# First weights between the quarters of the input, gate products behind the first pair: a start-up order of a DeltaNet and attention trunk on one core

## Chip, core and metric

The kernel runs on one core of a Trainium2 chip. The metric is the device time of one execution in microseconds; three runs of the kernel before gave a median of 649.35 us (648.83 to 649.79).

## What is computed

Two decoder layers over 256 tokens of width 1024, all in float32. Layer 0 mixes tokens with a gated DeltaNet, layer 1 with attention; each is followed by a squared-ReLU MLP. The change lies in the first sub-layer, whose beginning is:

```
def gated_deltanet(hn, w_in, conv_w, a_log, dt_bias, out_norm_g, w_out):   # hn = rmsnorm(x, g)
    proj = hn @ w_in                                                       # 1024 -> 4*1024 + 16
    qkv = silu(causal_depthwise_conv(proj[..., :3 * 1024], conv_w))
    z = proj[..., 3 * 1024:4 * 1024]
    b_raw, a_raw = proj[..., 4096:4104], proj[..., 4104:]                  # 8 heads each: the gates
    q, k = l2norm(heads of qkv) ...
    beta = sigmoid(b_raw); g = -exp(a_log) * softplus(a_raw + dt_bias)
    o = chunk_gated_delta_rule(q, k, v, g, beta)                           # decay = exp of differences of cumsum(g)
    o = rmsnorm(o, out_norm_g) * silu(z)
    return o @ w_out
```

## The kernel before

**Weights.** All large matrices lie in HBM as one stream of 200 units of 128x1024 floats (512 KB), in the order in which they are used. `prep(u)` (L105) loads a unit into one of three buffers `wf` from SyncE's queue, then ScalarE rounds it to `wh` (L115, "cast") and VectorE forms the rest `wl = wf - wh` (L116, "split"). The first eight units are loaded, cast and split in halves. `wh` and `wl` have five buffers each. A buffer `wf` is loaded again once its split is done, so unit u+3 is issued behind the split of unit u; a buffer `wh` is cast again once TensorE has used it, so the cast of unit u+5 waits for the products of unit u.

**Products.** `mm3` (L128) makes each float32 product of three TensorE products: wh*xh, wh*xl, wl*xh. The input is h0 (x transposed: 8 blocks of 128 features by 256 tokens, loaded in four quarters of two blocks). `Norm.feed` (L166) makes of one quarter, with the norm's weight, `n_h` (ScalarE, L169) and `n_l` (VectorE, L170), squares it (ScalarE, L174 or L177) and adds the square to `n_acc` (VectorE, L178). `Norm.finish` (L180) sums `n_acc` on TensorE (`n_ps`), takes the inverse root in small VectorE steps down to `n_col` (L189), and spreads it over the partitions by TensorE (`n_pb`) and ScalarE (`n_bc`). The norm's factor is applied behind the projections, so the products needn't wait for it.

**A pair.** `pair` (L196) projects 256 output columns, one head's k and q, from two units: 48 products into one PSUM bank. Pairs share the three "acc" banks. What follows for head n (`do_kq`, L499) is the convolution: VectorE multiplies the bank by `n_bc` into `cin` (L478, which frees the bank), ScalarE makes the first tap (L482), VectorE the other three for two blocks (six operations at L484); then a tanh or SiLU, four transposes on TensorE (`kqt`, L517) and squares on ScalarE (L519). `project_gates` (L387) makes the 16 gate columns of plain float32 products of h0 (`ba_ps`, L395), and `make_gates` (L400) the decays of them, by some 25 small VectorE operations. `head_decay` (L453) makes a head's decay matrix: two VectorE operations `ms` (L463), three TensorE transposes `row`, three exponentials.

**Order.** Two strings set the order of the program. `START` (L44) is the order of the first loads, preps and feeds: a token of two signs is a load and its queue (p = `par`, the small parameters; b = `wba`, the gate weights; c = the first constants, with the identity; 0 to 3 = quarters of x; s = SyncE's queue, a = ScalarE's), w is `prep` of the next unit, f is `feed` of the next quarter. `ORDER` (L47) is the order of the mixer's steps: G gates' products, N norm, M gates, L and C two later loads of constants (`sel` and the rest of `con`), kn a pair's products, Kn its convolution, Dn a decay, then v, z, u, i, r, o. The pair k5 comes second and its convolution K5 far behind, so that its bank is held and the others go round in two. From this program a scheduler sets the order of each engine's instructions; every engine then works in its order, and waits in place.

Of the kernel before, what the change touches and what calls it, by code (L numbers as in the profile page):

```python
# [40 lines left out]
}  # L41


START = "pa 0s 1s 2s 3s ba f f w w f f ca"  # L44


ORDER = (  # L47
    "G L k0 N k5 M K0 k3 D0 k2 K2 k1 D6 D2 K3 k4 D1 K1 s0 u2 u0 D3 k6 C K4 D4 D7 u3 u1 K6 i0 k7 K5 K7 v1 "
    "s1 u4 u6 D5 u5 u7 z0 i1 v0 r0 v3 o0 v2 r1 z1 o1"
)  # L50

# [24 lines left out]
def trunk_kernel(ctx: ExitStack, tc: tile.TileContext, xT, wst, wba, par, con, selc, gfin, out):  # L76
# [293 lines left out]
    nprep = nfeed = 0  # L370
    for st in START.split():
        if st == "w":
# [595 lines left out]
```

## Time and profile before

| | |
|---|---|
| median of three runs | 649.35 us |
| the profiled execution | 651.13 us, of which 649.3 us span |
| TensorE busy | 634.4 us, 98% of the span, granted clock 0.996 |
| VectorE busy | 453.7 us, 70%; 8 tenths or more in every slice from 16 to 146 us |
| ScalarE busy | 345.1 us, 53% |
| chain that ended last | TensorE 85%, VectorE 5%, ScalarE 5%, DMA 4%, issue 1% |
| HBM read | 107.51 MB, 167 GB/s over the span |

Busy shares are over the whole span; the change lies in its first tenth. A TensorE row can be "busy" while it waits inside a pipelined stretch, so in that tenth the reader should go by start times and by what ended each idle time. In timelines the bracket behind a row gives the engine's idle time before it, and what released it.

### The profile page before, as it was taken

How to read it: one execution, taken by the hardware profiler on the slowest of the kernel's cores; microseconds unless marked ns; L12 is line 12 of the kernel's file. 1: busy time of each engine (PE TensorE's matmuls, PEld its weight loads, DVE VectorE, ACT ScalarE, POOL GpSimd, SP SyncE). 2: the span in 40 equal slices, each digit the busy share in tenths (PEclk: the TensorE clock that was granted, in tenths of full speed). 3: DMA queues.
4: the chain of work that ended last, by engine and by line, in shares of the span. 5: the costliest groups of instructions: out<-in, count | busy, mean ns of one | idle time of the engine just before them, and what ended most of it. 6: DMA issues, size and time to landing. Idle time of an engine off the chain costs nothing.

```text
span 649.3 us, 13944 instructions
## 1 busy us (share of the span) xinstructions
PE 634.4 (98%) x5754; PEld 608.5 (94%) x5754; DVE 453.7 (70%) x841; ACT 345.1 (53%) x570; POOL 4.0 (1%) x10
## 2 busy tenths in 40 slices
PE   8999999999999999999999999999999999999995
PEld 6988887978999999999999999889999999999995
DVE  5999998997797666645554757775877776545443
ACT  6679873463566666634443444552656555434331
POOL 1000000000000000000000000000000000000000
PEclk9999999999999999999999999999999999999998
DMA  7754253252456565666565655555556666556641
GB/s 259 238 187 130 66 163 100 68 163 66 152 160 185 195 194 195 193 196 194 195 195 195 190 166 163 162 163 162 157 160 204 196 196 195 163 195 195 195 132 65
DMA packets 32031, 109.46 MB, mean 169 GB/s; under 512 B 3552, under 2 KB 3936, under 8 KB 31968
## 3 DMA queue, kind: packets, MB, share of 16 engines
q1 hardware_dynamic: 31248, 107.71, 52.5%
q8 instruction: 45, 0.74, 0.5%
q10 hardware_dynamic: 720, 0.86, 0.4%
q14 instruction: 18, 0.15, 0.1%
HBM read 107.51 MB, written 1.05 MB: 167 GB/s over the span
## 4 chain that ended last, share of the span: by engine, by line
PE 85%; DVE 5%; ACT 5%; DMA 4%; issue 1%; ACTq 0%; DVEq 0%
PE ps_last L136 12%; PE ps_up_m L132 8%; PE ps_up_m L133 8%; PE ps_up_m L130 8%; PE ps_dn_m L133 4%; PE ps_dn_m L132 4%; PE ps_dn_m L130 4%; PE ps_vn L136 3%; DMA wf<-in_w 3%; PE ps_z L136 3%; DVE wl L116 2%; PE ps_qk L132 2%; PE ps_qk L133 2%; PE ps_qk L130 2%; ACT wh L115 2%; PE kk L136 2%
## 5 line engine op out<-in xcount | busy, mean ns | idle before, releaser
L116 DVE TENSOR_TENSOR wl<-wf,wh 128x1024 fp32r<-128x1024 f32 (+1 forms) x208 | 244.3, 1182 | 141.0 <-ACT wh L115 140.4
L115 ACT CAST wh<-wf 128x1024 fp32r<-128x1024 f32 (+1 forms) x208 | 209.7, 1017 | 235.8 <-PE ps_up_m L132 63.7
L130 PE MATMUL ps_up_m<-n_h,wh 128*128 128x256 f32 x512 | 141.6, 277 | 0.5 <-ACT n_h L169 0.5
L132 PE MATMUL ps_up_m<-n_l,wh 128*128 128x256 f32 (+1 forms) x516 | 141.9, 276 | 0.0
L133 PE MATMUL ps_up_m<-n_h,wl 128*128 128x256 f32 x512 | 141.8, 277 | 0.0
L130 PEld LDWEIGHTS ps_up_m<-n_h,wh 128*128 128x128 f32 x512 | 96.1, 188 | 0.7 <-ACT n_h L169 0.7
L132 PEld LDWEIGHTS ps_up_m<-n_l,wh 128*128 128x128 f32 x516 | 96.6, 188 | 0.0
L133 PEld LDWEIGHTS ps_up_m<-n_h,wl 128*128 128x128 f32 x512 | 96.1, 188 | 0.0
L130 PE MATMUL ps_dn_m<-hh_m,wh 128*128 128x256 f32 x256 | 70.7, 276 | 0.0
L132 PE MATMUL ps_dn_m<-hl_m,wh 128*128 128x256 f32 x256 | 70.7, 276 | 0.0
L133 PE MATMUL ps_dn_m<-hh_m,wl 128*128 128x256 f32 x256 | 70.7, 276 | 0.0
L136 PE MATMUL ps_last<-wl,hh_m 128*128 128x256 f32 x226 | 61.9, 276 | 0.0
L136 PE MATMUL ps_last<-wh,hl_m 128*128 128x256 f32 x224 | 61.9, 276 | 0.0
L136 PE MATMUL ps_last<-wh,hh_m 128*128 128x256 f32 x224 | 61.8, 276 | 0.0
L130 PEld LDWEIGHTS ps_dn_m<-hh_m,wh 128*128 128x128 f32 x256 | 48.0, 188 | 0.0
L132 PEld LDWEIGHTS ps_dn_m<-hl_m,wh 128*128 128x128 f32 x256 | 48.0, 188 | 0.0
L133 PEld LDWEIGHTS ps_dn_m<-hh_m,wl 128*128 128x128 f32 x256 | 48.0, 188 | 0.0
L136 PEld LDWEIGHTS ps_last<-wl,hh_m 128*128 128x128 f32 x226 | 42.3, 188 | 0.0
L136 PEld LDWEIGHTS ps_last<-wh,hh_m 128*128 128x128 f32 x224 | 42.1, 188 | 0.0
L136 PEld LDWEIGHTS ps_last<-wh,hl_m 128*128 128x128 f32 x224 | 42.0, 188 | 0.0
L130 PE MATMUL ps_kq<-n_h,wh 128*128 128x256 f32 x128 | 36.6, 286 | 0.0
L130 PE MATMUL ps_qk<-n_h,wh 128*128 128x256 f32 x128 | 36.3, 284 | 0.0
(278 smaller groups left out, 1292.1 us busy)
## 6 DMA issues: line engine op xcount, KB each, us to landing
wf<-in_w SPq DMA_DIRECT2D x192, 512.0 KB, 3.5
wf<-in_w SPq DMA_DIRECT2D x16, 256.0 KB, 4.2
h<-in_x SPq DMA_DIRECT2D x4, 256.0 KB, 6.5
gf<-in_g SPq DMA_DIRECT2D x1, 512.0 KB, 4.0
out<-hg SPq DMA_DIRECT2D x2, 256.0 KB, 2.1
out<-hg ACTq DMA_DIRECT2D x2, 256.0 KB, 2.5
sel<-in_sel SPq DMA_DIRECT2D x1, 448.0 KB, 4.9
cn<-in_con SPq DMA_DIRECT2D x1, 276.0 KB, 4.9
```

What stands on the lines that cost most here:

```text
L115: nc.scalar.copy(wh[:, s], wf[:, s])
L116: nc.vector.tensor_sub(wl[:, s], wf[:, s], wh[:, s].bitcast(F32))
L130: nc.tensor.matmul(o, wh, xh, start=start, stop=False, skip_group_check=True)
L132: nc.tensor.matmul(o[:, s], wh, xl[:, s], start=False, stop=False, skip_group_check=True)
L133: nc.tensor.matmul(o, wl, xh, start=False, stop=stop, skip_group_check=True)
L136: nc.tensor.matmul(o, l, r, start=start, stop=stop, skip_group_check=True)
```

## The change

The first two units are prepared between the quarters of x: load quarter 0, unit 0, quarter 1, feed both, unit 1, then quarters 2 and 3. The first constants move from ScalarE's queue to SyncE's, behind x. In `ORDER` the pair k0 comes before the gates' products G, the norm N follows G, and the load L of `sel` stands behind k5.

```
-START = "pa 0s 1s 2s 3s ba f f w w f f ca"
+START = "pa ba 0s w 1s f f w 2s 3s f f cs"
 ORDER = (
-    "G L k0 N k5 M K0 k3 D0 k2 K2 k1 D6 D2 K3 k4 D1 K1 s0 u2 u0 D3 k6 C K4 D4 D7 u3 u1 K6 i0 k7 K5 K7 v1 "
+    "k0 G N k5 L M K0 k3 D0 k2 K2 k1 D6 D2 K3 k4 D1 K1 s0 u2 u0 D3 k6 C K4 D4 D7 u3 u1 K6 i0 k7 K5 K7 v1 "
     "s1 u4 u6 D5 u5 u7 z0 i1 v0 r0 v3 o0 v2 r1 z1 o1"
 )
```

The scheduler moves more than the strings show. On SyncE's queue, from its first load (wf_111 and wf_96 are unit 0 before and now, h_72 is x), before:

```order
L114 DMA wf_111<-in_w 128x512
L379 DMA h_72<-in_x 128x512 x4
L114 DMA wf_111<-in_w 128x512
L114 DMA wf_120<-in_w 128x512 x2
L742 DMA sel<-in_sel 128x896
L114 DMA wf_165<-in_w 128x512 x2
```

and now:

```order
L114 DMA wf_96<-in_w 128x512
L379 DMA h_72<-in_x 128x512
L114 DMA wf_96<-in_w 128x512
L379 DMA h_72<-in_x 128x512
L114 DMA wf_118<-in_w 128x512 x2
L379 DMA h_72<-in_x 128x512 x2
L379 DMA cn<-in_con 128x384
L114 DMA wf_152<-in_w 128x512 x2
```

The last quarter of x was the fifth load of this queue and is now the eighth; the first constants follow it, and unit 2 (wf_165 before, wf_152 now) follows them without `sel` ahead.

On VectorE, from the split of unit 10 (wl_486) to the multiplications that free the banks of k3 (ps_kq_411) and k2 (ps_kq_483), before:

```order
L116 TENSOR_TENSOR wl_486<-wf_484,wh_485 128x1024
L431 SCALAR_TENSOR_TENSOR gt_p<-gt_p,gt_z 128x16
L478 TENSOR_TENSOR cin_147<-ps_kq_411,n_bc 128x2x256
L433 SCALAR_TENSOR_TENSOR gt_u<-gt_p,gt_u 128x16
L437 SCALAR_TENSOR_TENSOR gt_g<-gt_u,ea 128x16
L116 TENSOR_TENSOR wl_516<-wf_514,wh_515 128x1024
L442 COPY gt_gc<-gc_ps 128x16
L478 TENSOR_TENSOR cin_148<-ps_kq_483,n_bc 128x2x256
```

and now, from the same split on (wl_516, wl_570 and wl_600 are units 11 to 13, L510 with th_554 is head 2's):

```order
L116 TENSOR_TENSOR wl_486<-wf_484,wh_485 128x1024
L116 TENSOR_TENSOR wl_516<-wf_514,wh_515 128x1024
L478 TENSOR_TENSOR cin_148<-ps_kq_483,n_bc 128x2x256
L463 TENSOR_SCALAR ms_629<-cn,gt_gc 128x128
L116 TENSOR_TENSOR wl_570<-wf_568,wh_569 128x1024
L484 SCALAR_TENSOR_TENSOR y_kq_545<-cin_148,pm,y_kq_545 128x256 x6
L463 TENSOR_SCALAR ms_629<-cn,gt_gc 128x128
L463 TENSOR_SCALAR ms_639<-cn,gt_gc 128x128
L116 TENSOR_TENSOR wl_600<-wf_598,wh_599 128x1024
L510 SCALAR_TENSOR_TENSOR kq_386<-th_554,y_kq_545 128x2x128 x2
L463 TENSOR_SCALAR ms_639<-cn,gt_gc 128x128
L478 TENSOR_TENSOR cin_147<-ps_kq_411,n_bc 128x2x256
```

Before, k3's bank was freed first, one small step behind the split of unit 10; now k2's is, right behind the split of unit 11, and k3's comes behind head 2's convolution. The rest of the gates' chain (L431 to L442) and the decay of head 0 now stand ahead of this piece. On TensorE the pair k1 (ps_kq_567), which follows k2's, took k3's bank before and takes k2's now.

On TensorE the end of k2's pair now reads:

```order
L136 MATMUL gc_ps<-gt_g,cn 128x16
L132 MATMUL ps_kq_483<-n_l,wh_309 128x256
L133 MATMUL ps_kq_483<-n_h,wl_310 128x256
L130 MATMUL ps_kq_483<-n_h,wh_309 128x256
L517 MATMUL kqt_402<-cn,kq_386 128x128
L136 MATMUL gl_ps<-gt_gc,cn 128x8
L132 MATMUL ps_kq_483<-n_l,wh_309 128x256
L133 MATMUL ps_kq_483<-n_h,wl_310 128x256
L130 MATMUL ps_kq_483<-n_h,wh_309 128x256
L517 MATMUL kqt_402<-cn,kq_386 128x128 x3
L464 MATMUL row_474<-cn,ms_473 128x128 x2
L465 MATMUL row_474<-cn,gt_gc 128x128
```

Eleven products of k2 and then those of k1 follow. Before, kqt_402 stood some 16 products earlier than gc_ps, and gl_ps and row_474 stood within k1.

## Rows read from the trace of the kernel before

**Rows 1.** Busy time in stretches of 8 us: PE, PEld, DVE, ACT, POOL, clock, DMA, GB/s.
```profile
0.00:8.00 8.00, 5.70 (x18) 3.95 (x20) 2.16 (x7) 3.69 (x7) 3.00 (x8) 1.00 0.68 210
8.00:16.00 8.00, 7.40 (x60) 6.03 (x58) 6.98 (x14) 7.33 (x17) 0.00 (x0) 1.00 0.88 306
```

**Rows 2.** What TensorE waited for in 0 to 200 us: us, times, longest.
```profile
PE kqt L517 <- DVE kq L510: 1.6, 2, 0.8
...
PE ps_z L136 <- DVE cin L478: 0.3, 1, 0.3
```

**Rows 3.** Timeline of TensorE, start: start, length, operation, [idle before <- releaser].
```profile
1.25 4.94 PE L136 MATMUL warm<-wu 128*128 128x256 f32 x12 [1.25 <-DVE wu L358]
9.71 0.63 PE L136 MATMUL ba_ps<-h,sz 128*32 128x256 f32 x4
10.27 0.39 PE L130 MATMUL ps_kq<-n_h,wh 128*128 128x256 f32 x1
16.03 0.95 PE L136 MATMUL n_ps<-ones,n_acc 128*128 128x1 f32 x8
```

**Rows 4.** Timeline of ScalarE, start.
```profile
3.83 0.62 ACT L115 CAST wh<-wf 128x512 fp32r<-128x512 f32 x1 [1.14 <-DMA wf<-in_w]
5.38 0.91 ACT L169 ACTIVATE n_h<-h,pm 128x256 fp32r<-128x256 f32 x2 [0.93 <-DMA h<-in_x]
7.84 0.91 ACT L169 ACTIVATE n_h<-h,pm 128x256 fp32r<-128x256 f32 x2 [1.04 <-DMA h<-in_x]
10.34 0.62 ACT L115 CAST wh<-wf 128x512 fp32r<-128x512 f32 x1 [0.67 <-DMA wf<-in_w]
```

**Rows 5.** DMA issues of 0 to 30 us: KB each, median us from issue to landing.
```profile
wf<-in_w SPq DMA_DIRECT2D x3, 512.0 KB, 4.4
...
cn<-in_con ACTq DMA_DIRECT2D x1, 192.0 KB, 7.2
```

**Rows 6.** Timeline of VectorE, 8 to 22 us.
```profile
8.39 0.88 DVE L170 SCALAR_TENSOR_TENSOR n_l<-h,pm,n_h 128x256 fp32r<-128x256 f32 x2 [1.38 <-ACT n_h L169]
14.59 0.69 DVE L178 TENSOR_TENSOR n_acc<-n_acc,n_sq 128x512 f32<-128x512 f32 x1
15.20 2.49 DVE L116 TENSOR_TENSOR wl<-wf,wh 128x512 fp32r<-128x512 f32 x4
21.68 0.16 DVE L189 TENSOR_SCALAR n_col<-n_y 128x2 f32<-128x2 f32 x1
```

**Rows 7.** Timeline of VectorE, 29 to 45 us.
```profile
29.35 1.21 DVE L116 TENSOR_TENSOR wl<-wf,wh 128x1024 fp32r<-128x1024 f32 x1
36.88 0.68 DVE L478 TENSOR_TENSOR cin<-ps_kq,n_bc 128x512 f32<-128x512 f32 x1
37.63 0.47 DVE L463 TENSOR_SCALAR ms<-cn,gt_gc 128x128 f32<-128x128 f32 x2
39.26 1.22 DVE L116 TENSOR_TENSOR wl<-wf,wh 128x1024 fp32r<-128x1024 f32 x1 [1.16 <-ACT wh L115]
40.41 2.46 DVE L484 SCALAR_TENSOR_TENSOR y_kq<-cin,pm,y_kq 128x256 f32<-128x256 f32 x6
43.92 0.75 DVE L510 SCALAR_TENSOR_TENSOR kq<-th,y_kq 128x256 f32<-128x256 f32 x2
```

**Rows 8.** Timelines of SyncE's queue and of ScalarE: unit 12's issue and cast.
```profile
32.28 0.33 SPq L114 DMA_DIRECT2D wf<-in_w  x1
...
38.18 1.05 ACT L115 CAST wh<-wf 128x1024 fp32r<-128x1024 f32 x1 [1.87 <-DMA wf<-in_w]
```

**Rows 9.** Timeline of TensorE: first of k1, first kqt of head 2, kqt of head 3.
```profile
36.10 0.28 PE L130 MATMUL ps_kq<-n_h,wh 128*128 128x256 f32 x1
44.39 0.33 PE L517 MATMUL kqt<-cn,kq 128*128 128x128 f32 x1 [0.80 <-DVE kq L510]
50.26 0.66 PE L517 MATMUL kqt<-cn,kq 128*128 128x128 f32 x4 [0.16 <-ACT kq L513]
```

**Rows 10.** Busy time and clock just behind TensorE's last product (columns as in Rows 1).
```profile
642.00:644.00 2.00, 0.00 (x0) 0.00 (x0) 1.93 (x12) 1.12 (x3) 0.00 (x0) 0.95 0.00 0
```

## Prediction

> **What bounds the kernel now.** I read the busy times by stretch first, then TensorE's waits, then the timelines of the first 52 us. After the start TensorE is never short of work for long: already in 8 to 16 us 7.40 of 8 us are busy [rows 1], and the largest named wait, for head results of VectorE, is two times 0.8 us [rows 2]. Its clock is at the upper of its two levels (1.00, 2.4 GHz) from the start. So the span is TensorE's work plus what it waits, and only two things can move it here: when it begins to work on weights, and new or vanished waits while VectorE and the transfers set the pace (up to about 50 us).
>
> The start [rows 3]: twelve warm-up rows until 6.19, gates' products whenever a quarter of x lands, and the first weight product at 10.27. From there 48 products take 5.76 us (0.12 each) and `n_ps` starts at 16.03. The early time is spent waiting for transfers: ScalarE waits 0.93, 1.04 and 0.67 us for x and for the second half of unit 0 [rows 4], VectorE 1.38 us behind it [rows 6].
>
> **Landing times.** Before, loads of 256 KB on SyncE's queue land in this order: unit 0's half by 3.83, quarters 0 and 1 by 5.38 and 7.84 [rows 4], quarter 3 by 9.71 [rows 3], unit 0's other half by 10.34 [rows 4]. That is 0.63 us a load at the end of the list, and more before it. The first constants, 192 KB on ScalarE's queue, were under way for 7.2 us of that time [rows 5]; at the 306 GB/s of 8 to 16 us [rows 1], taking them away gives about 0.6 us. By place in the queue, less that 0.6: now quarter 0 lands at 5.3, unit 0's second half at 7.2, quarter 1 at 8.5, unit 1 at 9.1 and 9.7, quarters 2 and 3 at 10.4 and 11.0. So the last quarter comes 1.3 us later than before. Bounds: 11.6 if the constants cost nothing, about 9.7 (as before) if bandwidth is spare.
>
> [...]
>
> **The head.** From quarter 1 on VectorE is dense. It starts on it when `n_h` is there, 0.55 after 8.5. Then, in the new order: three pairs of `n_l` (0.88 a pair, [rows 6]), three additions (0.61, start to start in [rows 6]), unit 1's two splits and unit 2's two (2.49 for four): 2.64 + 1.83 + 2.49 = 6.96, so unit 2 is split at 16.0. Before it was at 15.20 + 1.25 = 16.45. TensorE does the first 12 products from 6.2 and has 36 left from 9.1: 4.3 us, plus eight gate products. Those go at 0.24 to 0.31 each (two in 0.63, [rows 3]), 2.1 us, and before they were hidden in the waits for x. That makes 15.5 against 16.03. Both leads agree: **0.5 us**, with bounds of 0 (quarter 3 at 11.6) and 1.3 (at 9.7). The load of unit 5 waits for unit 2's split and `n_col` for unit 5's: 21.68 [rows 6] becomes 21.2. The moved `sel` and second constants leave the queue ahead of unit 2 and unit 4 and land long before use; I cost them at nothing, and should they delay unit 5 by their 448 KB, the 0.5 is gone.
>
> **The middle.** k1's pair began at 36.10 [rows 9], on k3's bank, free for some time. Now it needs k2's bank, which VectorE frees behind the split of unit 11. That multiplication (before at 36.88, done by 37.48) now has k3's multiplication (0.60) behind it instead of ahead, and head 0's two `ms` (0.47, at 37.63 before) ahead of it [rows 7]; with the lead of 0.5: 37.48 - 0.60 + 0.47 - 0.5 = 36.85. TensorE gets there earlier and waits, a new wait of about 1.3 us after a shorter one for `gc_ps`. But three `row` transposes and `gl_ps`, 0.5 us, now lie behind it. So at this point it is 36.85 - 36.10 - 0.5 = **0.25 us behind**: the lead is spent.
>
> Next, the wait for head 2 at 44.39 [rows 9]. Before, the chain there was unit 12: issued at 32.28, landed at 38.18, 5.9 us [rows 8], with unit 11 issued only 1.7 before it, behind unit 8's split. That split stood at 29.35 [rows 7] behind five taps of head 0 (0.40 each); now it stands ahead of all of them, so it is 2.0 + 0.5 us earlier, and unit 11 no longer shares the engines with unit 12. I take 4.2 us for unit 12, alone on its way, a little under the 4.4 that the first whole units took in the median [rows 5] (late bound 5.9, as before), issued by the lead at 32.0: landed 36.2. Then: cast 1.05 [rows 8] to 37.3, split 1.14 (start to start), taps 2.46, two `ms` 0.47, next split 1.14 [rows 7]: the head's last step begins at 42.5 and its first half ends at 42.9, against 43.92 + 0.38 = 44.3. TensorE's 46 products of k1 end at 36.85 + 5.5 = 42.35; it waits 0.55, 0.25 less than before. Then come 4 `kqt`, 2 products and 6 `row`, about 1.6 us, and k4's 48 products (5.6), which end at 50.1. Before, head 3's `kqt` (0.66, now behind) stood ahead of k4's last four products: without it and its wait of 0.16 these ended at 50.26 - 0.16 + 0.48 = 50.6 [rows 9]. The lead is **0.5 us** again, and VectorE, some 1.4 us ahead here, should spare part of the waits that came behind (that 0.16, and 0.3 at `ps_z` [rows 2]); I take 0.1 of them: **0.6 us**. Behind this TensorE is dense, and everything from the MLP on has the order it had; I cost it at nothing. Between, the small triangular inverse has fewer products between its steps; its cover is the same `z` products, and if it fails, each of seven steps costs some 0.15.
>
> **Sum.** The profiled execution took 651.13 us (span 649.3): 650.5 after the change. It lies 1.8 above the median, so I forecast 649.35 - 0.6 = 648.75, given as **648.7 us**, which is no change: 0.2%, 1.3 us, is about what a measurement of this kernel can tell.
>
> **Rivals.**
> - *The lead is kept* (chance 0.32). Quarter 3 lands as before (lead 1.3) and both waits of 0.8 for head results [rows 2] go, since VectorE starts each head earlier: 1.3 to 2.9 us, centre 2.1, 647.2. For it speaks that VectorE idles 1.16 at 39.26 for a transfer that is now issued earlier [rows 7]; against it, that TensorE reaches these points earlier too.
> - *The bank decides* (chance 0.15), slower. VectorE works in order, so if unit 10 or 11 is late, k2's bank is held behind its split and TensorE stands. The second constants (276 KB) now go ahead of unit 11. From k1's start at 38.4 on (1.5 us later than worked out, two splits' wait) the loss is over 1.3; I price it at 1.3 to 2.5, 651.0.
> - *The clock falls* (chance 0.03), slower. Between the first 12 products (done by 7.7) and quarter 1 TensorE stands some 1.4 us. In the trace it does nothing from 642 to 644 and is still granted 0.95 over these 2 us [rows 10]. Its waits for x before 10.27 cost nothing either (1.00 in both first stretches [rows 1]). If it fell to 1.2 GHz, 36 products would take 4.3 us more: 653. The Trainium skill ("TensorE: Matmul & The Clock Gate", section "What's actually happening") has the array throttled after an idle stretch until activity returns; by that rule the loss is this rival's, and the row says that so short a gap passes without it.
> - *It does nothing*: a pair contracts over all of x, so k0 can't end before the last quarter in either order. That is inside my forecast.
>
> **Numbers.** No change 0.50, the lead kept 0.32, bank or clock 0.18. The forecast's own range is 648.05 to 650.65. Eight in ten: from the middle of the first rival's span (646.8, a lead of 2.5) to the lower part of the second's (650.8). Faster by over 0.2%: 0.32; within: 0.50; slower: 0.18.
>
> **What would show it.** Right: first weight product near 6.2 to 6.5 us; `n_ps` near 15.5; `n_col` near 21.2; a wait of TensorE for VectorE's L478 before k1, near 35.5; unit 12 cast near 36.2; first `kk` near 50.1. Wrong: quarter 3's `n_h` before 10.5 and no wait at L478 (faster), k1 after 38.4 (slower), or a granted clock under 1.00 in the first 16 us.

## The result: slower by 4 to 5 us

The changed kernel takes 654.29 us in the median of four runs (653.22 to 654.57), the kernel before 649.52 us (648.83 to 649.79): a ratio of 1.0065, with a 95% interval of 1.0052 to 1.0078 (4.2 us by the ratio, 4.8 between the medians). I had forecast 648.7 us, no change, with 650.8 as the upper end. The profiled execution has a span of 652.3 us.

A second profile of the unchanged kernel (the first experiment below) lies closer to its median than the one that the prediction was read from: span 648.0 us against 649.3. Three columns are therefore compared, each figure the start of the row named:

| us | before, as read | before, second profile | after |
|---|---|---|---|
| first weight product (TensorE L130) | 10.27 | 9.51 | 5.82 |
| `n_ps` | 16.03 | 15.07 | 15.12 |
| `n_col` (VectorE L189) | 21.68 | 21.54 | 19.98 |
| first product of k3 | 23.17 | 23.03 | 22.07 |
| first product of k1 | 36.10 | 35.59 | 37.39 |
| first `kqt` of head 2 | 44.39 | 42.63 | 44.23 |
| first `kk` | 51.22 | 49.40 | 51.11 |
| first group's sums (VectorE L524) | 60.18 | 58.35 | 63.09 |
| first product of the MLP (`ps_up_m`) | 182.04 | 180.66 | 185.01 |
| from there to the end of the span | 467.3 | 467.3 | 467.3 |

Everything happens before the MLP. The change wins 1 us up to k3's pair, and then loses 5.3 against the second profile: 1 us early became 4.35 us late.

The timeline of TensorE after the change, which answers to [rows 3] (start, length, operation, in the bracket the idle time before it and what ended it):

```profile
5.82 0.47 PE L130 MATMUL ps_kq<-n_h,wh 128*128 128x256 f32 x1
...
8.62 0.38 PE L130 MATMUL ps_kq<-n_h,wh 128*128 128x256 f32 x1 [1.06 <-ACT n_h L169]
...
15.12 0.95 PE L136 MATMUL n_ps<-ones,n_acc 128*128 128x1 f32 x8
...
21.13 0.60 PE L136 MATMUL n_pb<-cn,n_col 128*128 128x128 f32 x4
...
32.72 0.37 PE L136 MATMUL gc_ps<-gt_g,cn 128*128 128x16 f32 x2 [1.42 <-DVE gt_g L437]
...
37.39 0.36 PE L130 MATMUL ps_kq<-n_h,wh 128*128 128x256 f32 x1 [1.24 <-DVE cin L478]
...
44.23 0.33 PE L517 MATMUL kqt<-cn,kq 128*128 128x128 f32 x1 [1.38 <-DVE kq L510]
...
53.26 0.60 PE L517 MATMUL kqt<-cn,kq 128*128 128x128 f32 x4
...
56.65 0.44 PE L464 MATMUL row<-cn,ms 128*128 128x128 f32 x2 [0.80 <-ACT kqt L519]
...
87.53 0.66 PE L517 MATMUL kqt<-cn,kq 128*128 128x128 f32 x4 [1.25 <-ACT kqt L519]
```

The first rows show the head as it was meant: products from 5.82 on, one short wait for the second quarter, `n_pb` without a wait. From 32 us on there are five waits in place, 6.1 us together. The same summed up, what TensorE waited for from 8 to 185 us (us, times, longest), first after:

```profile
PE gc_ps L136 <- DVE gt_g L437: 1.4, 1, 1.4
PE kqt L517 <- DVE kq L510: 1.4, 1, 1.4
PE kqt L517 <- ACT kqt L519: 1.3, 1, 1.3
PE ps_kq L130 <- DVE cin L478: 1.2, 1, 1.2
PE ps_kq L130 <- ACT n_h L169: 1.1, 1, 1.1
PE row L464 <- ACT kqt L519: 1.0, 2, 0.8
...
```

and in the second profile of before:

```profile
PE n_pb L136 <- DVE n_col L189: 0.7, 1, 0.7
PE py L136 <- issue: 0.4, 1, 0.4
PE kqt L517 <- DVE kq L510: 0.4, 1, 0.4
PE kk L136 <- ACT rv L660: 0.4, 1, 0.4
...
```

Of these the wait for `n_pb` was the largest, and the change did remove it. The account against the second profile: 1.42 + 1.24 + 1.38 + 0.80 + 1.25 = 6.1 of new waits, less the 0.7 that head results cost before (0.4, and 0.3 for head 3), less the lead of 1.0, is 4.4; measured at the MLP's first product, 4.35. The smaller waits of the two lists (1.4 us after, 1.1 before) are left out of it.

In the busy times by stretch (PE, PEld, DVE, ACT, POOL, clock, DMA, GB/s) it shows as lost TensorE time; after:

```profile
24.00:32.00 8.00, 7.30 (x65) 7.10 (x63) 7.61 (x27) 4.89 (x9) 0.00 (x0) 1.00 0.76 249
32.00:40.00 8.00, 6.04 (x51) 5.90 (x52) 6.41 (x15) 5.37 (x16) 0.00 (x0) 1.00 0.61 193
40.00:52.00 12.00, 10.62 (x89) 9.94 (x88) 11.29 (x28) 8.95 (x23) 0.53 (x1) 1.00 0.42 141
52.00:64.00 12.00, 11.17 (x88) 10.19 (x87) 9.76 (x25) 10.32 (x30) 0.52 (x1) 1.00 0.42 131
```

and before, second profile:

```profile
32.00:40.00 8.00, 7.78 (x65) 7.68 (x66) 7.79 (x21) 6.31 (x17) 0.00 (x0) 1.00 0.79 234
...
52.00:64.00 12.00, 12.00 (x104) 11.66 (x103) 11.78 (x40) 11.82 (x30) 0.52 (x1) 1.00 0.41 134
```

TensorE loses 1.7 us in 32 to 40 and 0.8 in 52 to 64. VectorE loses more, 1.4 and 2.0: it was itself kept waiting. The clock is 1.00 in all of them.

### The profile page after: what moved, and what is told of

It is laid out like the page before. It is cut to its first block, busy times and chain, and to the rows that moved or that the text cites. A ratio compares the mean times of both kernels' runs of the same rounds, so it can differ in the third digit from the quotient of the medians.

```text
span 652.3 us, 13946 instructions
## 1 busy us (share of the span) xinstructions
PE 633.2 (97%) x5754; PEld 607.4 (93%) x5754; DVE 454.4 (70%) x841; ACT 345.4 (53%) x570; POOL 4.0 (1%) x10
## 3 DMA queue, kind: packets, MB, share of 16 engines
HBM read 107.51 MB, written 1.05 MB: 166 GB/s over the span
## 4 chain that ended last, share of the span: by engine, by line
PE 84%; DVE 6%; ACT 5%; DMA 3%; issue 1%; SPq 0%; ACTq 0%; DVEq 0%
PE ps_last L136 12%; PE ps_up_m L132 8%; PE ps_up_m L133 8%; PE ps_up_m L130 8%; PE ps_dn_m L132 4%; PE ps_dn_m L133 4%; PE ps_dn_m L130 4%; PE ps_vn L136 3%; PE ps_z L136 3%; DVE wl L116 2%; PE ps_qk L132 2%; PE ps_qk L133 2%; DMA wf<-in_w 2%; PE ps_qk L130 2%; ACT wh L115 2%; PE ps_last_e L136 1%
## 5 line engine op out<-in xcount | busy, mean ns | idle before, releaser
L130 PE MATMUL ps_up_m<-n_h,wh 128*128 128x256 f32 x512 | 141.7, 277 | 0.5 <-ACT n_h L169 0.5
L130 PEld LDWEIGHTS ps_up_m<-n_h,wh 128*128 128x128 f32 x512 | 96.2, 188 | 0.7 <-ACT n_h L169 0.7
L130 PE MATMUL ps_dn_m<-hh_m,wh 128*128 128x256 f32 x256 | 70.7, 276 | 0.0
L130 PEld LDWEIGHTS ps_dn_m<-hh_m,wh 128*128 128x128 f32 x256 | 48.0, 188 | 0.0
L130 PE MATMUL ps_kq<-n_h,wh 128*128 128x256 f32 x128 | 36.4, 284 | 2.3 <-DVE cin L478 1.2
L130 PE MATMUL ps_qk<-n_h,wh 128*128 128x256 f32 x128 | 36.3, 284 | 0.0
```

Of the source, the lines that this page charges most:

```text
L130: nc.tensor.matmul(o, wh, xh, start=start, stop=False, skip_group_check=True)
```

## The experiments

Theory A, formed from these rows: the loss is not in the loads but in the order behind them. The strings only set steps; the scheduler then deals VectorE's and TensorE's instructions anew, and now k3's convolution stands behind head 2's, and `gc_ps` ahead of 17 products of k2, whose last half unit was split by 25.46 us, so that they could have run. Rivals: the new START costs by itself (B), the late gates' products do (C).

**A second profile of before.** No edit.

> The kernel before, unchanged, for a second profile. Theory A: the profiled execution shown of it (651.13 us) was late in one place, the load of unit 12 (landed at 38.18 us, 5.9 us under way), and TensorE's wait of 0.8 us for head 2 came from that; a second profile shows the cast of unit 12 near 37 us, that wait under 0.5, and a span near 647.8 us. Rival: that wait belongs to the kernel, and is there again.

Span 648.0 us; one time, 649.79 us. Unit 12 is cast at 35.71 us without a wait for its load (38.18 in [rows 8]); TensorE's wait for head 2 is gone (start 42.63), and of the rows of [rows 2] for `kqt` 0.4 us for head 0 is left. Theory A's reading holds in these two executions: the late load belonged to the first of them, and with it two figures from which I had worked out gains.

**One part undone at a time.** The token L back to the front:

```
-    "k0 G N k5 L M K0 ..."
+    "L k0 G N k5 M K0 ..."
```

> The change with one token moved back: L (the load of sel) stands first in ORDER, ahead of k0. The head keeps k0 ahead of the gates' products. By the order of the instructions this alone brings VectorE back to freeing k3's bank ahead of k2's, as before the change. Theory A (the tail's order decides: K3's convolution behind head 2's makes everything from head 3 to the inverse late): most of the loss goes, 648.5 to 650.5 us, first kqt of head 3 near 50 us. Theory B (the new start itself decides: constants and gate weights late): still 653 to 655 us. Theory C (the late gates' products decide): still 653 to 655 us.

652.24 us, ratio 1.0037 (1.0023 to 1.0051); the first `kqt` of head 3 comes at 51.12. The gates' products G back ahead of k0:

```
-    "k0 G N k5 L M K0 ..."
+    "G k0 N k5 L M K0 ..."
```

> The change with G (the gates' products) back ahead of k0 in ORDER; L stays behind k5. From k5 on the order is the change's. Theory A (the tail's order decides): as the change, 653.5 to 655 us. Theory B (the new start): also 653 to 655. Theory C (gates' products behind k0 make the gates' chain late, TensorE's wait of 1.4 us for gt_g at 32 us is the first sign): 649.5 to 651, and that wait gone.

654.83 us, ratio 1.0075 (1.0063 to 1.0088). START alone (ORDER as before):

```
 START = "pa ba 0s w 1s f f w 2s 3s f f cs"
-    "k0 G N k5 L M K0 ..."
+    "G L k0 N k5 M K0 ..."
```

> Only the START string changed, ORDER as before. VectorE frees k3's bank ahead of k2's, as before. Theory A: 648.5 to 650.5 us (a lead of about 1 us at the first pair, some of it lost later). Theory B (the new start itself costs): 653 to 655. Theory C: 649 to 650.5.

651.88 us, ratio 1.0034 (1.0021 to 1.0047). ORDER alone:

```
-START = "pa ba 0s w 1s f f w 2s 3s f f cs"
+START = "pa 0s 1s 2s 3s ba f f w w f f ca"
```

> Only the ORDER string changed, START as before. The scheduler puts the gates' products between the first 12 products of k0 and the other 36, and the rest stays as before, with k3's bank freed first. Theory A: 649 to 650.5 us, as before. Theory B: as before too. Theory C (late gates' products): 651 or more.

650.34 us, ratio 1.0008 (0.9999 to 1.0017).

The place of G is worth nothing, so theory C is out. Its trace says more: with G in front k3's pair begins 1.1 us later than after the change (23.16 against 22.07 us), but TensorE's wait for `gt_g` is 0.61 us instead of 1.42, and k1 begins only 0.3 later (37.66 against 37.39). What the head gains is waited away by then.

With the new START, moving L, a load of 448 KB that nobody waits for, costs 2 us: with L in front VectorE frees k3's bank first, with L behind k5 it frees k2's. That is theory A; later weights aren't the reason, for unit 5 is issued later in the faster of the two kernels (17.80 us against 15.43). By itself the place of L costs nothing measurable: ORDER alone has L behind k5 too, and there VectorE frees k3's bank first, then k2's:

```profile
34.44 0.68 DVE L478 TENSOR_TENSOR cin<-ps_kq,n_bc 128x512 f32<-128x512 f32 x1
...
36.81 0.68 DVE L478 TENSOR_TENSOR cin<-ps_kq,n_bc 128x512 f32<-128x512 f32 x1
```

It is the two strings together that bring k3's bank behind k2's. But START with the old order also costs 2 us, which theory A had put at nothing: theory B has its half, and the forecast of 648.5 to 650.5 for both kernels with L in front failed. In the kernel with L in front a part of the rest can be TensorE's clock, which fell in its profiled execution (last section); in START alone it stayed at 1.00 up to the MLP. Both traces show an order in this half, too: a small step of the norm, `n_ms`, between the halves of unit 2. VectorE's timeline in the kernel with START alone:

```profile
14.29 0.68 DVE L116 TENSOR_TENSOR wl<-wf,wh 128x512 fp32r<-128x512 f32 x1
16.88 0.16 DVE L186 TENSOR_SCALAR n_ms<-n_ps 128x2 f32<-128x2 f32 x1 [1.91 <-PE n_ps L136]
17.45 0.29 DVE L405 TENSOR_REDUCE ba<-ba_pt 128x32 f32<-128x128 f32 x1 [0.41 <-PE ba_pt L403]
17.66 1.28 DVE L116 TENSOR_TENSOR wl<-wf,wh 128x512 fp32r<-128x512 f32 x2
```

VectorE stands 1.91 us for TensorE's `n_ps` while the second half's split, already possible, waits behind. Unit 5, whose buffer that split frees, is issued at 18.37 us, against 15.76 in the second profile of before and 15.43 after the change. With L in front of the changed order the same wait is 1.30 us.

**That wait in START alone, taken away.** One more prep in START, ahead of the constants; the order is that of before but for L, which stands ahead of G:

```
-START = "pa ba 0s w 1s f f w 2s 3s f f cs"
+START = "pa ba 0s w 1s f f w 2s 3s f f w cs"
-    "k0 G N k5 L M K0 ..."
+    "L G k0 N k5 M K0 ..."
```

> Only the START string as in the change and one prep more in it (unit 2 ahead of the constants), ORDER nearly as before. In the kernel with the START string alone (651.9 us) VectorE waited 1.9 us for n_ps with unit 2's second split behind it, and unit 5 was issued at 18.4 us. Theory E (that wait in place is what START alone loses): unit 5 issued before 17 us, TensorE's wait for head 0 under 0.8 us instead of 1.6, 650 to 651.3 us. Rival F (the loss is elsewhere): 651.9 us or more.

654.01 us, ratio 1.0063 (1.0041 to 1.0085): a miss. Unit 5 is issued at 15.61 us, as meant, yet TensorE's wait for head 0 stays at 1.7 us and the first group's sums come at 65.66. The scheduler had dealt everything behind anew as well: VectorE still stands 1.32 us for `n_ps`, now behind both halves, and TensorE 1.05 us before `gl_ps`. So this run doesn't tell what the 1.91 us cost; what START alone loses is read from its trace and not shown by a run.

**The constants' queue.** `cs` back to `ca`:

```
-START = "pa ba 0s w 1s f f w 2s 3s f f cs"
+START = "pa ba 0s w 1s f f w 2s 3s f f ca"
```

> The change with the first constants back on ScalarE's queue. The order of the rest is nearly the change's. If these 192 KB delay x and the first weights as worked out ahead of the prediction, n_ps comes 0.6 us later, but the end hangs on other waits: 654 to 655 us. Rival: the constants' place on SyncE's queue costs the change something: 652 to 653.5.

654.43 us, ratio 1.0068 (1.0042 to 1.0095), as the change itself. The queue of these 192 KB plays no part in the loss. The last product of k0 starts at 15.26 instead of 15.01: 0.25 us, where I had worked out 0.6 for the landing of x. Its trace, and that of the kernel with G in front, lack the wait of 1.38 us for head 2 (first `kqt` at 43.15 and 43.44 us), so this term of the account above belongs to the profiled execution of the change, whose unit 12 came late; in the median both kernels are no faster for it.

**K3's place.** K3 directly behind K2:

```
-    "... k3 D0 k2 K2 k1 D6 D2 K3 k4 ..."
+    "... k3 D0 k2 K2 K3 k1 D6 D2 k4 ..."
```

> The change with K3 (head 3's convolution) directly behind K2 in ORDER. VectorE then frees k2's and k3's banks one behind the other and works on head 3's taps right behind head 2's, ahead of the splits of units 12 and 13. Theory A (head 3's late convolution makes the first group's chain late, 2 to 3 us of the loss): 651 to 653 us, first group's sums (L524) at 60 to 61 us instead of 63. Rival D (that chain has slack; what is lost, is lost to waits in the first 50 us): 654 us or more, as the splits come later.

657.96 us, ratio 1.0116 (1.008 to 1.0152): a miss, and the slowest of all in the median, with runs from 653.8 to 660.9. The first group's sums do come earlier (61.54 us), but two splits were pushed behind twelve taps, k1 still waits 1.2 us for k2's bank, and the last two pairs, k6 and k7, begin 1.2 us later than after the change (54.84 and 62.19 us against 53.61 and 61.03). On top of it TensorE's clock fell in the profiled execution (last section); the one run with a mean granted clock as high as 0.997 took 653.8, about the change's time. Then K3 ahead of k2, and K2 behind k1:

```
-    "... k3 D0 k2 K2 k1 D6 D2 K3 k4 ..."
+    "... k3 D0 K3 k2 k1 K2 D6 D2 k4 ..."
```

> The change with K3 ahead of k2 and K2 behind k1 in ORDER: VectorE frees k3's bank first, ahead of the splits of units 10 and 11, so k1 doesn't wait for k2's bank. Theory A: the wait of 1.2 us before k1 is gone and the first group's sums come earlier than 63 us: 650.5 to 653. Rival D (no gain from head 3's place beyond the bank): 653 to 654.

651.81 us, ratio 1.0026 (1.0013 to 1.0039). What TensorE waited for from 8 to 185 us:

```profile
PE gc_ps L136 <- DVE gt_g L437: 1.6, 1, 1.6
PE kk L136 <- ACT rv L660: 0.6, 1, 0.6
PE ps_kq L130 <- ACT n_h L169: 0.5, 1, 0.5
...
```

The wait for k2's bank and the two for `kqt` squares are gone, the sums come at 59.85, and 2.5 us of the change's loss are gone. The wait for `gt_g` is still there.

**And `gc_ps` later.** The same, with the gates' chain M one step later:

```
-    "k0 G N k5 L M K0 k3 D0 K3 k2 k1 K2 D6 D2 k4 ..."
+    "k0 G N k5 L K0 M k3 D0 K3 k2 k1 K2 D6 D2 k4 ..."
```

> The kernel with K3 ahead of k2 (651.8 us, TensorE's wait of 1.6 us for gt_g at the product gc_ps still in it), now with M (the gates' chain) behind K0 in ORDER, which puts gc_ps some 70 products later on TensorE. Theory A (each of the waits in place is lost time): that wait is gone and no other of its size comes, 650 to 651 us. Rival D (the decays and the scales of the first group come later by the same move): 651.5 to 653.5.

649.96 us against 650.15, ratio 0.9991 (0.9969 to 1.0013): as before the change. The waits from 8 to 185 us:

```profile
PE ps_z L136 <- issue: 0.7, 1, 0.7
PE ps_kq L130 <- ACT n_h L169: 0.7, 1, 0.7
...
PE gc_ps L136 <- DVE gt_g L437: 0.2, 1, 0.2
...
```

With the change's START, k0 ahead of G, L behind k5, and three steps moved, the whole loss is gone. M alone, from the change:

```
-    "k0 G N k5 L M K0 k3 D0 k2 ..."
+    "k0 G N k5 L K0 k3 M D0 k2 ..."
```

> The change with M two steps later in ORDER (behind K0 k3) and nothing else. The scheduler then frees k3's bank ahead of k2's, right behind head 0's taps, and puts gc_ps at the end of k1. Theory A (the late K3 and the early gc_ps are what the change loses by): no wait for gt_g, none before k1, 650 to 652 us. Rival D (the gates come too late for the first group's scales): 653 us or more.

654.06 us, ratio 1.0056 (1.0035 to 1.0078): a miss. The waits go as expected: through k4 its trace leads the second profile of before by 0.8 us, k3's bank is freed first, and no wait is left before k1. But the first group's sums come at 61.08, 2.7 us later than in that profile, so rival D, whose 653 or more the median meets, is not out. Most of the loss comes later in this execution, between 132 and 152 us, and most of that from the clock (last section). The nine runs lie from 651.8 to 657.3 us; four of the five with a mean granted clock of 0.996 or more took 652.4 or less. How much of the median is order and how much clock stays open.

**A milder start.** Old ORDER and constants' queue, unit 0 between the quarters 1 and 2:

```
-START = "pa ba 0s w 1s f f w 2s 3s f f cs"
+START = "pa ba 0s 1s w 2s 3s f f w f f ca"
-    "k0 G N k5 L M K0 ..."
+    "G L k0 N k5 M K0 ..."
```

> Old ORDER, constants on ScalarE's queue as before; in START unit 0 goes between the quarters 1 and 2 of x, unit 1 behind them, the gate weights first. From n_ps on the order of the engines is that of before. Theory A (the end hangs on the order of VectorE's work and on when unit 5 is issued, not on the first product): 649 to 650.5 us, no change that can be measured. Rival G (an earlier first pair carries its lead through as long as the order behind it is kept): 648 to 649.

650.26 us, ratio 1.001 (0.9994 to 1.0025): no change. k3's pair begins 0.6 us earlier than in the second profile of before, and at the MLP's beginning some 0.3 us is left. No version was found that beats the kernel before.

## Why the prediction was wrong, step by step

**The start: right, and larger.** I had the first weight product at 6.2 to 6.5 (5.82), a gap of 1.4 us for quarter 1 (1.06, at a clock of 1.00), `n_ps` near 15.5 (15.12) and `n_col` near 21.2 (19.98). The lead I took as 0.5, with 1.3 as the bound; it is 1.1 at k3's first product against [rows 3]'s execution (23.17, from the table), 0.96 against the second profile.

**The first waits of the middle: right in kind, sized too small.** I named the wait for k2's bank, 1.3 us (1.24), and k1 at 36.85 (37.39). The "shorter one for `gc_ps`" had no price; it was 1.42 us. The reason stands in the order: `gt_g` comes 2.2 us earlier than in the second profile (32.41 against 34.61), but TensorE's `gc_ps` was moved up further, from behind the 45th product of k2 to behind the 31st. Unit 12 I had at 36.2: issued at 32.0, 4.2 us on its way. It was issued at 32.52 and cast at 37.63 with a wait of 0.93 for its load, some 5 us on its way (cast at 36.54 and 36.84 without such a wait in the kernels with the constants or G put back); so head 2 at 44.23 instead of 42.9, and the first `kk` at 51.11 instead of 50.1.

**The step that failed** is the sentence "VectorE, some 1.4 us ahead here, should spare part of the waits that came behind", with "Behind this TensorE is dense ... I cost it at nothing". VectorE was not ahead there: it began head 2's last step at 43.76, not at the 42.5 worked out, against 43.92 in the profile as read and 41.97 in the second. Head 3's convolution, which the order of VectorE's instructions showed behind head 2's, was priced for TensorE only, as a `kqt` that no longer stands inside k4, and counted as a gain of 0.16. Its own chain I did not follow. VectorE after the change:

```profile
36.55 0.69 DVE L478 TENSOR_TENSOR cin<-ps_kq,n_bc 128x512 f32<-128x512 f32 x1
...
44.63 0.69 DVE L478 TENSOR_TENSOR cin<-ps_kq,n_bc 128x512 f32<-128x512 f32 x1
...
63.09 0.17 DVE L524 TENSOR_SCALAR ss<-ss 128x16 f32<-128x16 f32 x1
```

and in the second profile of before:

```profile
33.81 0.68 DVE L478 TENSOR_TENSOR cin<-ps_kq,n_bc 128x512 f32<-128x512 f32 x1
...
36.19 0.68 DVE L478 TENSOR_TENSOR cin<-ps_kq,n_bc 128x512 f32<-128x512 f32 x1
...
58.35 0.17 DVE L524 TENSOR_SCALAR ss<-ss 128x16 f32<-128x16 f32 x1
```

After the change k2's bank is multiplied at 36.55 and k3's at 44.63; before, k3's came first, at 33.81. Eleven microseconds later for head 3's input make its `kqt` 4.8 us later (53.26 against 48.43). The decay `row` of head 1 shares a PSUM bank with the `kqt` (role "pr"), so it waits 0.80 for ScalarE's squares of them, and the first group's sums, on which its scales and its inverse hang, come 4.7 us late. The run with K3 in front returns 2.5 us. Measured against the profile as read, TensorE was 1.0 us behind the forecast at the first `kk` (51.11 instead of 50.1) and 3.6 at the MLP's first product (185.01 instead of 182.04 - 0.6): 2.6 us arose behind the point from which I had cost it at nothing.

**The gains counted from one late load.** The wait of 0.8 for head 2 and the 5.9 us of unit 12 were counted as what the change would shorten. The second profile has neither (4.3 us from issue to landing there). That the profiled execution lay 1.8 us above the median was said in the prediction, but its excess was taken as spread evenly, while 1.3 us of it came in that one place (the gap between the first two columns of the table grows from 0.51 at k1 to 1.82 at the first `kk`), on which two terms rested. A slip in the range does not change the outcome: its lower end, 646.8, is called the middle of the first rival's span, but that middle is a lead of 2.1, 647.2.

**The rivals.** "The bank decides" had the sign and the wait, but by its own mark (k1 after 38.4) it did not happen: k1 began at 37.39, and its 651.0 was too low because it had no chain behind the bank. "The lead is kept" fell. "The clock falls" did not happen in the changed kernel: 1.00 from 0 to 96 us in every stretch.

What stays open: why the lead at k3's pair never reaches the end, even where the order is repaired. In the milder start (0.6 us) it is gone at head 0: `n_col` comes 0.84 us earlier than in the second profile (20.70), but VectorE then stands 0.99 us for a cast, which itself waits 1.13 us for a load, and multiplies k0's bank at 23.06 (22.98 before). In the repaired kernel (0.8 us) 0.4 is left at both groups' sums (57.96 and 88.41 against 58.35 and 88.81), and at the MLP it is 0.6 behind; no run separates what takes it there.

## What to carry to other kernels

When a scheduler sets the order, an edit of loads is an edit of every engine's order: follow each moved step to its last consumer on all engines (here head 3's convolution to the first group's sums), not only to the engine that is busiest. A wait in place costs what could have run behind it, so look for small instructions moved ahead of independent work (`gc_ps` ahead of 17 products, `n_ms` ahead of a split). And before counting a wait of the old profile as a gain, see in a second execution whether it is there at all.

## What the runs showed of the hardware

Behind some waits of TensorE in the middle of dense work its clock fell, behind others of the same length it did not. In the kernel with K3 in front TensorE waits 1.57 us before `gc_ps` (32.87), and the granted clock goes to the lower of its two levels (0.50, 1.2 GHz) behind it:

```profile
30.00:32.00 2.00, 1.30 (x12) 1.11 (x10) 2.00 (x8) 1.60 (x2) 0.00 (x0) 1.00 0.57 210
32.00:34.00 2.00, 1.13 (x9) 1.16 (x10) 1.69 (x7) 1.13 (x2) 0.00 (x0) 0.99 0.15 33
34.00:36.00 2.00, 2.00 (x11) 2.00 (x11) 2.00 (x5) 0.66 (x5) 0.00 (x0) 0.50 0.62 238
36.00:38.00 2.00, 2.00 (x14) 2.00 (x14) 1.55 (x3) 2.00 (x10) 0.00 (x0) 0.66 0.33 94
```

It came back by 38 us. At half the rate over 2.0 us and at 0.66 over the next 2.0, that is, as an estimate, 1.7 us of products lost: as much as the wait itself. The kernel with L in front of the changed order shows the same behind a wait of 1.72 us for head 0 (34.81), and again some 1.7 us lost:

```profile
32.00:34.00 2.00, 1.09 (x10) 0.89 (x8) 1.16 (x3) 1.58 (x2) 0.00 (x0) 1.00 0.82 252
34.00:36.00 2.00, 1.19 (x9) 1.12 (x10) 1.79 (x7) 0.83 (x1) 0.00 (x0) 1.00 0.84 285
36.00:38.00 2.00, 2.00 (x15) 2.00 (x14) 2.00 (x7) 1.83 (x8) 0.00 (x0) 0.70 0.72 217
38.00:40.00 2.00, 2.00 (x11) 2.00 (x11) 1.76 (x3) 2.00 (x8) 0.00 (x0) 0.50 0.54 137
40.00:42.00 2.00, 2.00 (x18) 2.00 (x17) 2.00 (x6) 0.78 (x2) 0.00 (x0) 0.94 0.81 225
```

But the kernel with unit 2 prepared in START has a wait of 1.66 us for head 0 (33.02), TensorE is as idle around it, and the clock stays at 1.00:

```profile
30.00:32.00 2.00, 1.36 (x12) 1.16 (x11) 2.00 (x5) 1.32 (x3) 0.00 (x0) 1.00 0.21 29
32.00:34.00 2.00, 0.98 (x8) 0.98 (x9) 2.00 (x7) 0.92 (x1) 0.00 (x0) 1.00 0.70 252
```

START alone (a wait of 1.57) and the change (1.42) stay at 1.00 as well. So the length of a wait does not tell by itself whether the clock falls, and these runs don't show what does. The kernel with M later shows the fall once more, in the solve of the second group:

```profile
142.00:144.00 2.00, 0.56 (x3) 0.56 (x4) 1.95 (x9) 0.00 (x0) 0.00 (x0) 0.89 0.00 0
144.00:146.00 2.00, 2.00 (x12) 1.25 (x11) 1.40 (x5) 1.31 (x2) 0.00 (x0) 0.50 0.04 8
146.00:148.00 2.00, 2.00 (x33) 1.84 (x31) 1.29 (x2) 0.95 (x3) 0.00 (x0) 0.50 0.00 0
148.00:150.00 2.00, 2.00 (x6) 1.27 (x4) 0.00 (x0) 0.20 (x1) 0.00 (x0) 0.50 0.47 150
```

Six microseconds at half rate cost, by the same estimate, 3.0 us, with 0.11 and 0.10 of the 2 us on either side 3.4. The kernel with K3 behind K2 had 0.65 and 0.50 from 102 to 106. The Trainium skill ("TensorE: Matmul & The Clock Gate", section "What's actually happening") describes just these two states, with the lower one after idling. The rows agree on the two levels. For an order they show that a wait that looks cheap can cost twice in one execution and once in another.
